# Low parts of the output weights by accumulating DMAs, token sums on VectorE, a third plain pair and more norm buffers in a hybrid attention/SSM/ConvFFN block on one Trainium2 core

## The chip, the cores and the metric

The kernel runs on one core of one Trainium2 chip. The metric is the device time of one execution in microseconds. The kernel before took 1517.89 us (median of three runs, 1514.3 to 1518.22); one further execution was taken with the hardware profiler, and all lines of the profile come from it. A difference under about 0.3% (4.5 us) cannot be told from no change for this kernel.

## The reference, cut to what matters

One layer over 16 meta tokens and 1024 sequence tokens of width 1024. The change lies in the second half: merging and output projection, second norm, and the first matrix of the gated ConvFFN.

```python
def _mixer(xn, ...):
    ...
    merged = g[..., :D_MODEL] * y_a + g[..., D_MODEL:] * y_s      # y_a = attention @ w_attn_out
    return merged @ w_o

def _conv_ffn(xn, w_up, conv_w, conv_b, w_down):
    hid = xn @ w_up                                   # 1024 -> 2 * 2816
    hp = jnp.pad(hid, ((0, 0), (CONV_WIDTH - 1, 0), (0, 0)))
    conv = conv_b + sum(hp[:, j:j + seq_len] * conv_w[j] for j in range(CONV_WIDTH))
    val, gate = jnp.split(conv, 2, axis=-1)
    return (jax.nn.silu(gate) * val) @ w_down

def reference(...):
    ...
    h = h + _mixer(_rmsnorm(h, norm_mix_g), ...)
    h = h + _conv_ffn(_rmsnorm(h, norm_ffn_g), ...)
    return _rmsnorm(h, norm_final_g)[:, N_META:]
```

## The kernel before, in words

**Split operands.** Everything is float32. A matrix operand is cut into a high part of reduced width (type `float32r`, written `hi`) and a low part `lo = x - hi`, and each product is three matmuls: hi·hi, hi·lo, lo·hi. A `hi` is a copy on ACT (or POOL); a `lo` is a subtraction of two SBUF tiles on VectorE (DVE) or POOL (`split_lo`, line 129), or else an ACT copy of `-hi` followed by a DMA from POOL's queue that adds the original from DRAM onto it (`lo_by_dma`, lines 133 to 136). All of the `split_lo` instructions carry line 129, all of those DMAs line 136, so they are told apart by tile names.

**Order of the work.** The program is written in a fixed order, and a scheduler that has a model of the engines orders the instructions of each engine from it. On the chip each engine takes its own list strictly in order: an instruction that waits holds back everything behind it on that engine. The same holds for the DMA queues of SP and POOL.

**Attention output and merge (lines 943 to 963).** For each of eight row blocks `i`, the weights of `w_attn_out` are split by `wchunk` (high part on POOL, line 149; low part on DVE) and multiplied with the attention output in three pieces of 342 tokens (lines 958 to 960). DVE multiplies with the gate (L961) and adds the SSM part (L962) into `merged[i]`, tile `mr`. After each block `out_forms` makes operands of the output projection.

**Output projection (lines 1008 to 1070).** `merged @ w_o` is done with seven half-size block products instead of eight (a Strassen-like scheme), in the order `p = 0, 4, 1, 5, 2, 3, 6`. Each product has four token blocks `t` of 12 matmuls of 512 columns (lines 1015 to 1017), `i` or `j` running over four row blocks of the operands. `out_weights` loads the weight combination of a product, 128 rows of 512 columns for each `j` (from `w_o` itself for p = 0, 4, 6; from tensors `to_d` in DRAM, summed earlier, for the others). `out_forms(p, j)` makes the four operand tiles of slot `j`: high and low part of the token side (`a`) and of the weight side (`b`). Before, all `lo` are subtractions: on POOL for p = 0, 4, 5 and on DVE for p = 1, 2, 3, 6. The slots are the eight quarters of the tiles `xhi` and `xlo` (p = 0, 5, 3 share `xhi`, p = 4, 2 share `xlo`) and four tiles `op` (p = 1, 6), so forms of a product can only be written when the product two or three places ahead has been read by PE. Small products for the two meta tokens (lines 994, 995) read the same weight slots. DVE adds each result from PSUM to `h2` or `u2` (L1021); after p = 2 POOL adds `u2` to three blocks of `h2` for each `t` (L1024).

**Second norm (`normed`, lines 1026 to 1031).** For each 128 tokens: square and sum on ACT (L170, the squares are written into the tile `xs`, of which there are two), a scale on DVE (L172), a power on POOL (L174), the product into `xs` on DVE (L179), eight transposes on PE (L187), high parts on ACT (L189), low parts on DVE (L129, `xlo<-sp` and `xlo<-tp`). Blocks 5 to 8 follow product 6's token blocks, then the meta rows (block 0), then blocks 1 to 4.

**Up projection.** The 22 pairs (a gate chunk and a value chunk of 128 columns of `w_up`) come in two kinds. `plain_pair` multiplies directly: 144 matmuls of about 342 columns (lines 1165 to 1167), accumulated in PSUM, evacuated by one ACT and two DVE instructions a piece (L1169, L1171) that apply the convolution's taps. Three banks are called `mm`, one `po`; a piece can start when an earlier piece has left its bank. Pair 0 is cut in two parts: first the tokens from 514 on (blocks 5 to 8), then the others. `block_pair` uses the seven-product scheme: 168 matmuls of 258 or 256 columns (lines 215 to 217) over sums of weight blocks, which POOL makes (`combine`, L1121), and over sums of token blocks. These token sums are made once (`xn_forms`, L1185 on POOL: high plus low part, 16 of them; then 16 subtractions, lines 254 to 258, and 16 low parts `t0l` to `t3l` on DVE) while plain pair 1 runs. Pairs 0, 1 and 21 are plain, 2 to 20 are block pairs. The conv outputs and `hid` go to DRAM and the down projection follows.

**Memory.** `pool` opens a stretch of SBUF on the left or the right side; a tile of a new pool waits for the last users of what lay there. `merged` and `wstream` (the `raw`, `whi`, `wlo` tiles) lie on the right and are closed after the last norm, where the pool `upw` of up-projection weights takes their place.

Of the kernel before, what the change touches and what calls it, by code (L numbers as in the profile page):

```python
# [19 lines left out]
P = 128  # L20
# [30 lines left out]
def block_kernel(ctx, tc, x, meta, g1, x0t, g1t, w_q, w_k, w_v, w_f, w_u, w_g, b_f, w_ao, lam_d, bw_d, cw_d,  # L51
# [86 lines left out]
    def wchunk(src, k, eng=None, act=False):  # L138
        raw = wp.tile([P, k, P], F, tag="raw", name="raw", padded_shape=[P, KD, P])
        ld = (GP if act else SY).dma_start(raw, src)  # L140
        if act:
            after(ld, late[0])
        hi = wp.tile([P, k, P], R, tag="whi", name="whi", padded_shape=[P, KD, P])
        lo = wp.tile([P, k, P], R, tag="wlo", name="wlo", padded_shape=[P, KD, P])
        if act:
            S.copy(hi, raw)
            lo_by_dma(lo, hi, src)
            return hi, lo
        GP.tensor_scalar(hi, raw, 1.0, 0.0, ALU.mult, ALU.add)
        split_lo(eng or V, lo, raw, hi)  # L150
        return hi, lo
# [25 lines left out]
    def norm_rows(pl, src, n, gB, xs):  # L177
        rs = norm_factor(pl, src, n, 3, xs)
        V.scalar_tensor_tensor(out=xs[:n], in0=src, scalar=rs[:n], in1=gB[:n], op0=ALU.mult, op1=ALU.mult)  # L179
# [708 lines left out]
    merged = [mp.tile([P, LQ], F, name=f"mr{i}") for i in range(KD)]  # L888
# [30 lines left out]
    def out_weights(p, q, pl, tag, bufs=2):  # L919

        t_ = pl.tile([P, 2, 512], F, tag=tag, name="wr", bufs=bufs)
        src = (o_block(*own_w[p]) if p in own_w else to_d[p])[256 * q:256 * q + 256]
        SY.dma_start(t_, src.rearrange("(c p) d -> p c d", p=P))
        wr[p, 2 * q], wr[p, 2 * q + 1] = t_[:, 0], t_[:, 1]

    def out_forms(p, j):
# [12 lines left out]
        for q, src in ((0, (a11, a11, a11, a21, a12, a22, a11)[p]), (2, wr.pop((p, j)))):  # L939
            S.copy(slot[q], src)  # L940
            split_lo(GP if p in (0, 4, 5) else V, slot[q + 1], src, slot[q])
# [6 lines left out]
    for i in range(KD):  # L948
# [5 lines left out]
        whi, wlo = wchunk(w_ao[i], 4)  # L954
# [80 lines left out]
    tags = {1: "raw", 5: "whi", 2: "wlo", 3: "raw", 6: "whi"}  # L1035
# [7 lines left out]

    operands(None)
# [29 lines left out]
    st_o.close()  # L1074
    st_w.close()
# [4 lines left out]

    st_r = ExitStack()
    fc = pool(st_r, "ffnc", side="right")

    cwt = fc.tile([P, 4, 2 * NFF], F, name="cwt")
    SY.dma_start(cwt, cwt_d)
# [7 lines left out]
    KH = KD // 2  # L1093
    rp = pool(st_r, "upw", side="right")
# [6 lines left out]

    def up_raw(m):
        raw = rp.tile([P, KD, P], F, tag="raw", name="raw", bufs=3)
        SY.dma_start(raw, w_up[m])
        return raw

    def ring():
        t_ = rp.tile([P, 2, KH, P], R, tag="sw", name="sw", bufs=8)
        return t_[:, 0], t_[:, 1]

    def split_q(src):
        hi, lo = ring()
        S.copy(hi, src)  # L1113
        split_lo(V, lo, src, hi)
        return hi, lo
# [34 lines left out]
    def plain_pair(c, parts=(QBLK,)):  # L1150
        res = []
        ws = {}
        for part, (m, tag) in ((part, mt) for part in parts for mt in ((NFF + c, "og"), (c, "ov"))):
            if m not in ws:
                raw = up_raw(m)
                ws[m] = [split_q(raw[:, KH * q:KH * q + KH]) for q in range(2)]
                res.append(conv_out(m, tag))
            w2, o = ws[m], res[len(ws) - 1 if len(ws) < 2 else int(m == c)]
# [23 lines left out]
    def xn_forms():  # L1182
        def whole(dst, r, h_, k):
            b = block(r, h_)
            GP.tensor_tensor(dst, b[0][:, k].bitcast(F), b[1][:, k].bitcast(F), ALU.add)  # L1185
# [7 lines left out]
    def block_pair(c):  # L1193
# [3 lines left out]
        down_weight_sums(c - 2, sums[n_])  # L1197
# [588 lines left out]
```

## Time and profile before

| | |
|---|---|
| Runs before, median of three | 1517.89 us (1514.3 to 1518.22) |
| Profiled execution, its time | 1517.67 us |
| Its span, first to last instruction | 1515.9 us |
| PE busy | 1447.7 us (96%) |
| DVE / ACT / POOL busy | 1093.1 / 697.6 / 782.2 us (72 / 46 / 52%) |
| Attention output and merge on PE | about 669 to 720 us |
| Output projection on PE | 719.7 to 810 us |
| Plain pairs 0 and 1 on PE | 811.7 to 882 us |
| Block pairs on PE | from about 882 us, 20.1 us each |

A row of the timeline reads: start, duration, engine, line, operation, out<-in, shape and type, how many were merged, and in brackets the idle time before it with what ended it. A row of the windows reads: the stretch, its length, then for each engine its busy time and the number of instructions, then the granted PE clock as a share of the full one, the mean busy share of the 16 DMA engines, and GB/s. Matmuls overlap in their recorded durations, so the pace of PE is read from starts or counts.

### The profile page before, as it was taken

The page shows a single profiled execution, that of the slowest core. Times are in us where ns is not written, and L with a number is a line of the kernel's source. Part 1 is how long each engine was busy: PE and PEld are TensorE (multiplying, and loading weights), DVE is VectorE, ACT ScalarE, POOL GpSimd, SP SyncE. Part 2 cuts the span into 40 slices and gives each one's busy share as a digit, 9 for nine tenths or more (in the row PEclk, how much of TensorE's full clock was granted, in tenths as well). Part 3 has the DMA queues.
Part 4 walks back from the last instruction along what each step waited for, and adds up shares of the span by engine and source line. Part 5 has one row for each costly group of instructions (what it writes and reads, how often), then busy time and mean ns, then how long its engine had stood idle before and what let it go on. Part 6 is the DMA issues. An engine that isn't in the chain of part 4 may idle for free.

```text
span 1515.9 us, 26588 instructions
## 1 busy us (share of the span) xinstructions
PE 1447.7 (96%) x9736; PEld 1363.6 (90%) x9736; DVE 1093.1 (72%) x2178; ACT 697.6 (46%) x1351; POOL 782.2 (52%) x866
## 2 busy tenths in 40 slices
PE   7999997999999999999998799999999999999997
PEld 6989997998999999998787799999999999878886
DVE  7878748871656676645777987888887774798785
ACT  6334665531546565540435444444444444444343
POOL 1411136760546555546852645555544326599766
PEclk9999999999999999999999899999999999999999
DMA  6365572551027422164533146676643214774413
GB/s 241 94 163 141 141 139 63 164 168 51 23 78 192 128 55 92 43 251 152 211 88 135 43 105 174 174 189 180 166 114 98 73 68 167 290 238 127 138 49 111
DMA packets 88150, 201.46 MB, mean 133 GB/s; under 512 B 14330, under 2 KB 25210, under 8 KB 87636
## 3 DMA queue, kind: packets, MB, share of 16 engines
q1 hardware_dynamic: 69956, 161.83, 32.7%
q0 software_dynamic: 11840, 27.28, 10.1%
q10 hardware_dynamic: 6224, 10.65, 1.9%
q8 instruction: 77, 1.26, 0.3%
q14 instruction: 53, 0.43, 0.1%
HBM read 160.65 MB, written 69.35 MB: 152 GB/s over the span
## 4 chain that ended last, share of the span: by engine, by line
PE 78%; DVE 9%; DMA 6%; issue 3%; POOL 2%; ACT 2%; SPq 0%; POOLq 0%; DVEq 0%; ACTq 0%
PE mm L155 4%; PE mm L157 4%; PE mm L156 4%; PE sp L215 4%; PE sp L216 4%; PE sp L217 4%; PE mm L215 3%; PE tp L215 3%; PE mm L217 3%; PE tp L216 3%; PE mm L216 3%; PE tp L217 3%; PE tp L752 2%; PE po L774 1%; PE po L773 1%
## 5 line engine op out<-in xcount | busy, mean ns | idle before, releaser
L155 PE MATMUL mm<-xhi,whi 128*128 128x342 f32 (+2 forms) x488 | 159.4, 327 | 1.0 <-DVE q L129 1.0
L157 PE MATMUL mm<-xhi,wlo 128*128 128x342 f32 (+2 forms) x488 | 158.3, 325 | 0.0
L156 PE MATMUL mm<-xlo,whi 128*128 128x342 f32 (+2 forms) x488 | 157.7, 324 | 0.0
L1144 POOL TENSOR_TENSOR ov<-ov,og 128x1024 f32<-128x1024 f32 x21 | 51.3, 2441 | 130.7 <-ACT og L1143 127.9
L129 DVE TENSOR_TENSOR sw<-sf,sw 128x512 fp32r<-128x512 f32 x76 | 70.7, 931 | 52.5 <-ACT sw L1113 52.5
L1113 ACT CAST sw<-sf 128x512 fp32r<-128x512 f32 x76 | 47.5, 625 | 112.1 <-POOL sf L1121 79.2
L155 PEld LDWEIGHTS mm<-xhi,whi 128*128 128x128 f32 x488 | 91.9, 188 | 2.1 <-PE sp L710 0.8
L157 PEld LDWEIGHTS mm<-xhi,wlo 128*128 128x128 f32 x488 | 91.8, 188 | 0.3
L156 PEld LDWEIGHTS mm<-xlo,whi 128*128 128x128 f32 x488 | 91.9, 188 | 0.2
L217 PE MATMUL mm<-xhi,sw 128*128 128x256 f32 (+1 forms) x304 | 85.5, 281 | 0.0
L215 PE MATMUL mm<-xhi,sw 128*128 128x256 f32 (+1 forms) x304 | 85.3, 281 | 0.0
L216 PE MATMUL mm<-xlo,sw 128*128 128x256 f32 (+1 forms) x304 | 85.2, 280 | 0.0
L759 ACT CAST th<-tp 128x256 fp32r<-128x256 f32 (+3 forms) x120 | 56.2, 472 | 61.8 <-PE tp L752 28.1
L129 DVE TENSOR_TENSOR tl<-tp,th 128x256 fp32r<-128x256 f32 (+3 forms) x120 | 65.2, 547 | 25.8 <-ACT th L759 24.4
L724 POOL TENSOR_SCALAR pt<-pt,nm 128x144 f32<-128x144 f32 (+4 forms) x72 | 51.6, 729 | 50.7 <-DVE nm L723 49.7
L1121 POOL TENSOR_TENSOR sf<-raw,sf 128x512 f32<-128x512 f32 x38 | 62.2, 1638 | 27.4 <-DVE sw L129 27.4
L1206 DVE SCALAR_TENSOR_TENSOR ov<-hv,cwt,ov 128x1024 f32<-128x1024 f32 x38 | 74.2, 1953 | 0.2
L1121 POOL TENSOR_TENSOR sf<-raw 128x512 f32<-128x512 f32 x38 | 49.9, 1314 | 45.9 <-DVE sw L129 21.7
L1113 ACT CAST sw<-raw 128x512 fp32r<-128x512 f32 x69 | 42.4, 620 | 58.9 <-PE sp L217 27.8
L722 ACT ACTIVATE pt<-pt,nm 128x144 f32<-128x144 f32 (+4 forms) x72 | 52.9, 735 | 27.3 <-DVE nm L721 26.9
L715 DVE CUSTOM_DVE_ANT_0 pt<-sp,fb 128x328 f32<-128x328 f32 (+8 forms) x112 | 46.4, 430 | 19.5 <-PE sp L710 11.3
L129 DVE TENSOR_TENSOR sw<-raw,sw 128x512 fp32r<-128x512 f32 x69 | 57.6, 842 | 3.5 <-ACT sw L1113 2.6
(693 smaller groups left out, 5733.9 us busy)
## 6 DMA issues: line engine op xcount, KB each, us to landing
raw<-in_w_up_dram SPq DMA_DIRECT2D x44, 512.0 KB, 3.7
t_d<-in_w_dn_dram POOLq DMA_DIRECT2D x44, 256.0 KB, 6.9
ar<-a_d SPq DMA_DIRECT2D x44, 256.0 KB, 4.9
wr<-t_d SPq DMA_DIRECT2D x44, 256.0 KB, 2.9
a_d<-ov SPq DMA_DIRECT2D x21, 512.0 KB, 2.6
wr<-in_w_dn_dram SPq DMA_DIRECT2D x33, 256.0 KB, 3.4
t_d<-in_w_dn_dram SPq DMA_DIRECT2D x22, 256.0 KB, 4.7
t_d<-t_d SPq DMA_DIRECT2D x22, 256.0 KB, 4.7
```

Of the source, the lines that this page charges most:

```text
L129: return eng.tensor_tensor(out_, src, hi.bitcast(F), ALU.subtract)
L155: yield PE.matmul(ps, whi[:, i, :], ahi[:, i], start=(i == 0), stop=False)
L156: yield PE.matmul(ps, whi[:, i, :], alo[:, i], start=False, stop=False)
L157: yield PE.matmul(ps, wlo[:, i, :], ahi[:, i], start=False, stop=(i == k - 1))
L215: PE.matmul(ps, a[0][:, i], bh, start=(i == 0 and not joins), stop=False, skip_group_check=True)
L216: PE.matmul(ps, a[0][:, i], bl, start=False, stop=False, skip_group_check=True)
L217: PE.matmul(ps, a[1][:, i], bh, start=False, stop=(i == kh - 1), skip_group_check=True)
L722: S.activation(pt[:n, :kc], pt[:n, :kc], AF.Exp, bias=nm[:n, 1:2], scale=0.125, accum_out=nm[:n, 2:3])
L759: S.copy(th[:kn, z:tw], tp[:kn, z:tw])
L1113: S.copy(hi, src)
L1121: sums.append(GP.tensor_tensor(f_, a, b, op))
L1206: V.scalar_tensor_tensor(out=o, in0=h_[:, j:SEQ + j], scalar=cwc(j, m), in1=o, op0=ALU.mult, op1=ALU.add)
```

## The change

1. **Low parts of the output weights.** In `out_forms` the low part of the weight side (`slot[3]`) is no longer a subtraction but `lo_by_dma`: an ACT copy of `-hi` and an accumulating DMA of 256 KB in POOL's queue, from `w_o` or `to_d`. There are 28 of each (seven products, four `j`).
2. **High parts of `w_attn_out`** are copied by ACT instead of POOL (`copy=True`), the low parts stay on DVE.
3. **Norm buffers.** The squares go into a tile of their own (`sf`, two), the result of the meta rows is written in place, and the results of blocks 7 and 2 go into the third `raw` buffer of the up weights.
4. **First pair's weights ahead.** `merged` and `wstream` are closed before product 2 and `upw` is opened there; the weights of pair 0 are loaded and split in that place.
5. **Token sums** (`whole`) run on DVE, not on POOL.
6. **Pair 2 is a plain pair;** the block pairs are 3 to 20, and the sums of the down weights follow one pair later (`c - 3`).

```diff
-    def wchunk(src, k, eng=None, act=False):
+    def wchunk(src, k, eng=None, act=False, copy=False):
...
+        if copy:
+            S.copy(hi, raw)
+            split_lo(V, lo, raw, hi)
+            return hi, lo
         GP.tensor_scalar(hi, raw, 1.0, 0.0, ALU.mult, ALU.add)
         split_lo(eng or V, lo, raw, hi)
...
-    def norm_rows(pl, src, n, gB, xs):
-        rs = norm_factor(pl, src, n, 3, xs)
+    def norm_rows(pl, src, n, gB, xs, sq=None):
+        rs = norm_factor(pl, src, n, 3, sq)
...
-        for q, src in ((0, (a11, a11, a11, a21, a12, a22, a11)[p]), (2, wr.pop((p, j)))):
-            S.copy(slot[q], src)
-            split_lo(GP if p in (0, 4, 5) else V, slot[q + 1], src, slot[q])
+        a_ = (a11, a11, a11, a21, a12, a22, a11)[p]
+        S.copy(slot[0], a_)
+        split_lo(GP if p in (0, 4, 5) else V, slot[1], a_, slot[0])
+        b_, src = wr.pop((p, j))
+        S.copy(slot[2], b_)
+        lo_by_dma(slot[3], slot[2], src)
...
-        whi, wlo = wchunk(w_ao[i], 4)
+        whi, wlo = wchunk(w_ao[i], 4, copy=True)
...
     def normed(c, dst, n):
-        xs = n2.tile([P, D], F, tag="xs", name="xs", bufs=2)
-        norm_rows(n2, dst, n, g2B, xs)
+        if c:
+            pl, tag, bufs = (rp, "raw", 3) if c in (7, 2) else (n2, "xs", 2)
+            xs = pl.tile([P, D], F, tag=tag, name="xs", bufs=bufs)
+        else:
+            xs = dst
+        sq = rp.tile([P, D], BF, tag="sf", name="sq", bufs=2)
+        norm_rows(n2, dst, n, g2B, xs, sq)
...
     for p in (0, 4, 1, 5, 2, 3, 6):
+        if p == 2:
+            st_o.close()
+            st_w.close()
+            fc = pool(st_r, "ffnc", side="right")
+            cwt = fc.tile([P, 4, 2 * NFF], F, name="cwt")
+            rp = pool(st_r, "upw", side="right")
+            early = {m: pair_weights(m) for m in (NFF, 0)}
+            SY.dma_start(cwt, cwt_d)
         for t in range(4):
             out_product(p, t)
...
         def whole(dst, r, h_, k):
             b = block(r, h_)
-            GP.tensor_tensor(dst, b[0][:, k].bitcast(F), b[1][:, k].bitcast(F), ALU.add)
+            V.tensor_tensor(dst, b[0][:, k].bitcast(F), b[1][:, k].bitcast(F), ALU.add)
...
-        down_weight_sums(c - 2, sums[n_])
+        down_weight_sums(c - 3, sums[n_])
...
-    plain_pair(0, ([(514, 256), (770, 254)], [(0, 258), (258, 256)]))
+    plain_pair(0, ([(514, 256), (770, 254)], [(0, 258), (258, 256)]), early)
     xn_forms()
     plain_pair(1)
-    for c in range(2, NFF - 1):
+    plain_pair(2)
+    for c in range(3, NFF - 1):
         block_pair(c)
```

How the order of instructions moves, at three places. The line numbers of the changed kernel are 4 to 21 higher (L1021 is L1029, L1024 is L1032, L1171 is L1191, L1185 is L1205).

DVE in the output projection, from the last result of product 4 to the first results of product 1 (`h<-h,sp`); `xlo` are the low parts of product 2's operands, `mr` its token side and `wr` its weight side. Before:

```order
L129 TENSOR_TENSOR xlo<-mr_8510,xlo 128x512
L1021 TENSOR_TENSOR h_9082<-h_9082,po 128x512
L129 TENSOR_TENSOR xlo<-mr_8511,xlo 128x512
L129 TENSOR_TENSOR xlo<-wr,xlo 128x512 x4
L1021 TENSOR_TENSOR h_9082<-h_9082,sp 128x512
```

In the changed kernel:

```order
L1029 TENSOR_TENSOR h_9090<-h_9090,po 128x512
L1007 TENSOR_TENSOR ml<-ml,tp 2x512
L129 TENSOR_TENSOR xlo<-mr_8510,xlo 128x512
L129 TENSOR_TENSOR xlo<-mr_8511,xlo 128x512
L1029 TENSOR_TENSOR h_9090<-h_9090,sp 128x512
```

The four weight-side subtractions no longer stand ahead of the first result of product 1.

POOL after product 5, where product 3's weight sides are made (`to_d_85` is the weight combination of product 3) and `u` is added to `h`. Before, POOL had only the twelve additions there:

```order
L1000 TENSOR_TENSOR hm<-hm,ml 2x512
L1024 TENSOR_TENSOR h_9082<-h_9082,u_9076 128x512 x6
L1024 TENSOR_TENSOR h_9082<-h_9082,u_9077 128x512 x6
```

In the changed kernel:

```order
L136 DMA xhi<-to_d_85 128x512 x2
L1032 TENSOR_TENSOR h_9090<-h_9090,u_9084 128x512 x3
L136 DMA xhi<-to_d_85 128x512 x2
L1032 TENSOR_TENSOR h_9090<-h_9090,u_9084 128x512 x3
L1032 TENSOR_TENSOR h_9090<-h_9090,u_9085 128x512 x6
```

The DMAs for `j` = 2 and 3 stand behind three additions that need the first result of product 2.

DVE at the end of the norm: the last low parts of block 4, then the evacuation of pair 0's first part, the piece `og 128x256` being the one whose bank the second part takes first (two instructions of that form empty it). Before:

```order
L129 TENSOR_TENSOR xlo<-tp,xhi 128x4x128
L1171 SCALAR_TENSOR_TENSOR og<-mm,cwt,og 128x256
L1171 SCALAR_TENSOR_TENSOR og<-mm,cwt,og 128x254
L1171 SCALAR_TENSOR_TENSOR og<-mm,cwt,og 128x256
```

In the changed kernel:

```order
L129 TENSOR_TENSOR xlo<-tp,xhi 128x4x128
L1205 TENSOR_TENSOR fa<-xhi,xlo 128x514
L1205 TENSOR_TENSOR fb<-xhi,xlo 128x514
L1205 TENSOR_TENSOR fa<-xhi,xlo 128x514
L1191 SCALAR_TENSOR_TENSOR og<-mm,cwt,og 128x256
L1205 TENSOR_TENSOR fa<-xhi,xlo 128x514 x2
L1191 SCALAR_TENSOR_TENSOR og<-mm,cwt,og 128x254
L1191 SCALAR_TENSOR_TENSOR ov<-mm,cwt,ov 128x256
L1191 SCALAR_TENSOR_TENSOR ov<-po,cwt,ov 128x254
L1191 SCALAR_TENSOR_TENSOR og<-mm,cwt,og 128x256
```

Five token sums and three other evacuations now stand ahead of the instruction that frees that bank. Further on, PE has 18 matmuls of the first block pair's second product (`sp`) between the first and the second value piece of plain pair 1, that is before plain pair 2.

More of the change, by code (lines that the diff above doesn't have):

```diff
@@ L887, in block_kernel @@
     mp = pool(st_o, "merged", side="right")
[L888 removed]
+    merged = [mp.tile([P, LQ], F, tag=f"mr{i}", name=f"mr{i}") for i in range(KD)]
     st_m = ExitStack()
@@ L1034, in block_kernel, with up_raw, ring, split_q @@
     after_of = {None: (1,), 0: (5,), 4: (2,), 5: (3, 6)}
-    tags = {1: "raw", 5: "whi", 2: "wlo", 3: "raw", 6: "whi"}
+    def up_raw(m):
+        raw = rp.tile([P, KD, P], F, tag="raw", name="raw", bufs=3)
+        SY.dma_start(raw, w_up[m])
+        return raw
+    def ring():
+        t_ = rp.tile([P, 2, KH, P], R, tag="sw", name="sw", bufs=8)
+        return t_[:, 0], t_[:, 1]
+    def split_q(src):
+        hi, lo = ring()
+        S.copy(hi, src)
+        split_lo(V, lo, src, hi)
+        return hi, lo
+    def pair_weights(m):
+        raw = up_raw(m)
+        return [split_q(raw[:, KH * q:KH * q + KH]) for q in range(2)]
+    tags = {1: "raw", 5: "whi", 2: "wlo", 3: "raw", 6: "wlo"}
     def operands(p):
```

35 lines of the change are left out of this document (9 added, 26 removed).

## Prediction

> **What bounds the kernel now.** I read the page first, then the chain and the waits of PE over the stretch that the change touches (685 to 900 us), then windows with the granted clock, then the timelines of DVE, POOL and ACT around each wait.
>
> ```profile
> span 1515.9 us, 26588 instructions
> PE 1447.7 (96%) x9736; PEld 1363.6 (90%) x9736; DVE 1093.1 (72%) x2178; ACT 697.6 (46%) x1351; POOL 782.2 (52%) x866
> ```
>
> PE is busy for all but 68 us, so only what removes a wait of PE, or its matmuls, shortens the time. In the stretch of the change PE waited four times over 1 us:
>
> ```profile
> PE mm L1165 <- DVE og L1171: 11.2, 2, 8.5
> PE mm L958 <- POOL whi L149: 3.4, 1, 3.4
> PE sp L1015 <- DVE h L1021: 2.8, 1, 2.8
> PE sp L187 <- DVE xs L179: 2.6, 1, 2.6
> ```
>
> Behind each, PE ran slowly (next to last three columns: granted clock, DMA share, GB/s):
>
> ```profile
> 690.00:694.00 4.00, 4.00 (x18) 3.85 (x19) 3.65 (x4) 0.62 (x1) 2.19 (x3) 0.64 0.23 67
> 757.00:762.00 5.00, 5.00 (x16) 3.92 (x17) 3.55 (x6) 2.98 (x6) 1.27 (x1) 0.66 0.08 21
> 834.00:840.00 6.00, 5.82 (x28) 5.85 (x29) 4.84 (x9) 0.98 (x2) 4.57 (x5) 0.53 0.01 3
> 872.00:877.00 5.00, 4.95 (x17) 4.98 (x18) 4.64 (x8) 2.07 (x4) 4.42 (x4) 0.50 0.29 47
> ```
>
> Length times the missing clock is what each cost besides the wait: 1.4, 1.7, 2.8 and 2.5 us. So there are 20.0 us of waits and 8.4 us of slow clock, 28.4 us, to win at most.
>
> **The long wait: token sums beside plain pair 1.** DVE works on the token forms while PE wants its banks emptied:
>
> ```profile
> 853.03 0.68 DVE L257 TENSOR_TENSOR fa<-fa 128x514 f32<-128x514 f32 x1
> 853.63 0.68 DVE L129 TENSOR_TENSOR t0l<-fa,t0h 128x514 fp32r<-128x514 f32 x1
> ...
> 865.35 1.75 DVE L257 TENSOR_TENSOR fa<-fa 128x514 f32<-128x514 f32 x1
> ```
>
> POOL's timeline after the first place and at the second:
>
> ```profile
> 856.98 1.69 POOL L1121 TENSOR_TENSOR sf<-raw,sf 128x512 f32<-128x512 f32 x1 [4.82 <-DVE sw L129]
> ...
> 864.83 3.40 POOL L1185 TENSOR_TENSOR fa<-xhi,xlo 128x514 f32<-128x514 f32 x2
> ```
>
> The same subtraction takes 0.68 us at 853, the next starting 0.60 us after it, while POOL is idle (4.82 us before 856.98); and it takes 1.75 at 865, where POOL's sums run. Only behind such rows comes the evacuation that PE waits for. On DVE alone the 16 sums cost about 16 × 0.6 = 9.6 us, and the 32 subtractions beside them come at the short pace. With 16 + 32 at 0.6 (29 us), 8 weight splits at 0.6 (4.8) and the evacuations left of pairs 0 and 1 (about 10), DVE needs some 44 us. The PE work beside it now includes plain pair 2, so I take the wait of 8.5 and its 2.5 us of slow clock as gone: **11.0 us** (8 to 11). That there is cover: the forms are done about 20 us before the first full block product. But 18 of its matmuls stand ahead inside plain pair 1, where the third quarter of one token form is due; by my sum DVE and PE get there within 1 us of each other, so each microsecond of lateness there is a wait.
>
> **The third plain pair.** PE's timeline has the pace of a plain pair, ACT's timeline and the view of line 224 that of the block pairs:
>
> ```profile
> 878.24 0.32 PE L1165 MATMUL mm<-xhi,sw 128*128 128x342 f32 x1
> ...
> 880.12 0.32 PE L1165 MATMUL mm<-xhi,sw 128*128 128x342 f32 x1
> ```
> ```profile
> 885.42 0.37 ACT L224 COPY c<-mm 128x256 f32<-128x256 f32 x1 [0.64 <-PE mm L217]
> ```
> ```profile
> L224 ACT COPY c<-mm x12: 352/370/375, 884.4 to 985.7; 128x258 f32<-128x258 f32 x6, 128x256 f32<-128x256 f32 x6
> ```
>
> Twelve matmuls of 342 take 1.88 us, 0.157 each; 144 take 22.6. Two copies L224 belong to each block pair, so from the second to the twelfth lie five pairs: (985.7 − 885.4) / 5 = 20.1 us. The swap costs **2.5 us** (2 to 3), on PE's path with no cover.
>
> **The norm.** Before, the last low part of block 4 came at 832.9 and the first bank of pair 0 was emptied by three evacuations after it:
>
> ```profile
> 832.17 0.69 DVE L129 TENSOR_TENSOR xlo<-tp,xhi 128x512 fp32r<-128x512 f32 x1 [0.16 <-ACT xhi L189]
> 832.78 1.25 DVE L1171 SCALAR_TENSOR_TENSOR og<-mm,cwt,og 128x256 f32<-128x256 f32 x3
> ```
>
> PE's side: the start of pair 0 in the timeline, four transposes in the chain, and a window of its matmuls:
>
> ```profile
> 811.67 0.36 PE L1165 MATMUL mm<-xhi,sw 128*128 128x258 f32 x1
> ```
> ```profile
> 801.08 0.44 PE tp L187 x4
> ```
> ```profile
> 810.00:820.00 10.00, 10.00 (x86) 9.67 (x85) 6.43 (x12) 5.49 (x12) 1.09 (x2) 1.00 0.16 66
> ```
>
> With the squares in a tile of their own ACT no longer waits for `xs`, and four weight splits fewer lie ahead, so the transposes reach PE in time. From 811.7, PE has 96 matmuls at 10 / 86 = 0.117 (11.2 us) and 4.2 us of transposes (32 at 0.11, and 8 short ones): it runs dry at 827.1. The last transposes stand 16 matmuls earlier, 825.2; an ACT copy and a DVE subtraction of some 0.6 each end at 826.5. Then the list has five token sums (5 × 0.6) and five evacuations (5 × 1.25 / 3 = 2.1): the bank is free at 831.6, not at 834.0. So of the two waits (2.6 and 2.7) one of 4.5 is left, with the clock's 2.8, and pair 0's second part starts **2.4 us** earlier (0 to 8, the upper end if no wait is left).
>
> **The output projection.** The 2.8 us wait came from DVE:
>
> ```profile
> 749.34 6.86 DVE L129 TENSOR_TENSOR xlo<-wr,xlo 128x512 fp32r<-128x512 f32 x4
> 756.12 0.67 DVE L1021 TENSOR_TENSOR h<-h,sp 128x512 f32<-128x512 f32 x1
> ```
>
> Those four are now DMAs, so this wait and its clock, 4.5 us, go. What is late next is product 3. Its slots are free when product 5 ends; call that 0. Rows for the chain are a window of the matmuls, two copies of ACT, POOL's additions, and the landing times of accumulating DMAs by line (L136, then L1139):
>
> ```profile
> 770.00:780.00 10.00, 10.00 (x46) 8.29 (x45) 7.19 (x12) 5.41 (x10) 2.94 (x3) 1.00 0.39 116
> ```
> ```profile
> 770.22 0.62 ACT L940 CAST xhi<-mr 128x512 fp32r<-128x512 f32 x1 [6.74 <-PE tp L1016]
> 770.75 0.62 ACT L940 CAST xhi<-wr 128x512 fp32r<-128x512 f32 x1
> ```
> ```profile
> 777.06 18.70 POOL L1024 TENSOR_TENSOR h<-h,u 128x512 f32<-128x512 f32 x12 [18.25 <-DVE u L1021]
> ```
> ```profile
> L136 POOL DMA_DIRECT2D wlo<-in_w_g_dram x7: 862/872/1222, 73.1 to 171.4; - x7
> ...
> DMA to landing us min/median/max: 6.3/7.3/13.1
> ```
> ```profile
> DMA to landing us min/median/max: 4.8/6.9/8.9
> ```
>
> PE reaches product 3 after product 2 (48 matmuls and 8 small ones at 0.22, four of them done earlier): about 12.0, and its slot `j` = 2 at 13.4. ACT's twelve operations at 0.53 start about 1.5 early and end at 4.8. On POOL the three additions wait for product 2's first result, 4.7, and take 3 × 1.56 or less: the DMA for `j` = 2 is issued at 8.6 to 9.4. The last landing row is that of the accumulating DMAs of 256 KB into DRAM (L1139, 4.8 to 8.9, median 6.9); the row above it is of 512 KB into SBUF (7.3). Mine are 256 KB into SBUF: 4.8 at best, 6.9 at worst in a quiet queue. They land at 13.4 to 16.3: a wait of 0 to 3 us, with clock 0 to 5. Taken: 1.6 and 0.4 for the clock, near the short end, since the queue is quiet there. Product 5's land by then; its `j` = 3 within 1 us. **2.5 us** gained (−3 to 4.5). The 28 `-hi` copies of ACT (28 × 0.53 = 15 us) lie in its idle time, 46% busy, and cost nothing by themselves.
>
> Two rules beside these rows. The Trainium skill, "SBUF — State Buffer", section "SBUF: two separate sides", warns that a DMA issued from GpSimd cannot write its descriptors while VectorE runs an instruction in a two-port mode; the trace has 0.87 us for the median issue and 1.22 for the longest (row L136), so hardly any of it. By that rule each of the two late DMAs would stand for one DVE instruction of 0.6 us, and the gain would be 1.2 us smaller. The Trainium skill, "TensorE: Matmul & The Clock Gate", section "What's actually happening", has the clock halved after at least one idle window of about 3.4 us; the trace differs, 0.66 after a wait of 2.8. By that rule the wait at product 3 costs no clock, and the gain is 0.4 us larger.
>
> **The attention output.** PE waited for POOL's `whi` (the second row of the waits), which stood in POOL's list behind weight-side subtractions; they ended at 688.05:
>
> ```profile
> 684.30 3.75 POOL L129 TENSOR_TENSOR xlo<-wr,xlo 128x512 fp32r<-128x512 f32 x3
> ```
>
> The window just before, and POOL's DMA queue on the page (packets, MB, share):
>
> ```profile
> 676.00:680.00 4.00, 4.00 (x27) 4.00 (x26) 1.49 (x3) 1.76 (x3) 4.00 (x4) 1.00 1.04 401
> ```
> ```profile
> q0 software_dynamic: 11840, 27.28, 10.1%
> ```
>
> Both leave POOL. But the new copy stands in ACT's list behind the copies of the fourth load `wr`, and here all 16 DMA engines are full. A megabyte of POOL's queue costs 0.101 × 1515.9 / 27.28 = 5.6 us of all engines; four new DMAs (1.05 MB) are 5.9 us. They can push that load, and with it the copy, back by up to 5.9 us. Of 3.4 + 1.4 = 4.8 us I take **3.0** (0 to 4.8).
>
> Edits with one answer: weights of pair 0 ahead (DVE split them during the last products before, too), meta rows in place, and `down_weight_sums` one pair later, which still ends two pairs before the last: zero. The scheduler also reorders some of the down projection's operands; I take zero and widen the range by 2.
>
> **The sum.** 11.0 + 2.4 + 2.5 + 3.0 − 2.5 = 16.4 us. Against the profiled execution's own 1517.67 (span 1515.9 and 1.8 around it; 0.2 under the median) this is **1501.3 us**.
>
> **The rivals.**
>
> *Late DMAs.* If they land in 10 us rather than 5 to 6 (13.1 is the longest row above, in full engines), product 3 waits 5 us more, product 5 about 3, the attention output wins nothing: 16.4 − 11 = 5.4, **1512 us**. For it: engines full at 676. Against: a share of 0.39 at 770. Chance 0.15.
>
> *DVE becomes the bound: slower.* If the short pace at 853 had another cause than POOL's silence, each token operation takes up to the 1.75 of the row at 865, 1.1 more; I take 0.8. Of the 48, 37 stand ahead of the 18 matmuls inside plain pair 1 in DVE's list: 37 × 0.8 = 30 us late there, PE's list is in order, and the cover of pair 2 comes behind it. Net 16.4 − 30 = −14: **1531 us**. It decides from a delay of 16.4 us there, 0.44 for each of the 37. Against: at 853 DVE ran at 0.60 while POOL had nothing, and that is the state the change makes. Chance 0.05.
>
> *More than forecast.* If evacuation and sums fall the other way on DVE and no wait is left in the norm, and product 3's DMAs are in time: + 5 + 2 + 1.5, **1492 us**. Chance 0.14.
>
> *The change does not do what it says,* that is, waits move one for one (a wait at product 3, one before the second part of pair 0, one at the 18 matmuls): **1517 us**. Chance 0.04.
>
> **How the numbers follow.** The forecast has 0.62, its own range being 1496 to 1507. Range of 8 in 10: it and the larger part of 1492 and 1512: 1493 to 1511. About 0.3%, 4.5 us, is what a measurement can tell from no change. Faster by more than that: 0.62 + 0.14 + most of the late DMAs 0.12 = 0.88. Same: 0.04 + 0.03 = 0.07. Slower: 0.05.
>
> **What would show it.** Right: no wait of PE on `og` over 5 us in plain pairs 0 to 2, full-width DVE subtractions there at 0.6 us apart, none at `h<-h,sp`, a wait of 0 to 3 us at the start of product 3 on a DMA, one of about 4 before the second part of pair 0, the first block pair about 6 us later than the first one before, though one pair further on. Wrong: a clock of 0.5 in plain pair 1, or PE waiting for `t1l`, or `whi` late again at 686.

## The result, and the profile after

The changed kernel takes 1506.4 us median against 1518.1 before, a ratio of 0.9931 (95% interval 0.9909 to 0.9952). Measured again beside the first experiments it was 1508.5 against 1516.1, 0.9962 (0.9949 to 0.9975). So it is faster by 7.6 to 11.7 us, where 16.4 were forecast. Its page begins:

```profile
span 1503.6 us, 26570 instructions
PE 1447.3 (96%) x9712; PEld 1364.3 (91%) x9712; DVE 1058.6 (70%) x2173; ACT 713.6 (47%) x1384; POOL 746.8 (50%) x854
```

PE's waits in the stretch of the change (640 to 930 us):

```profile
PE mm L966 <- ACT whi L150: 5.9, 1, 5.9
PE mm L1185 <- DVE og L1191: 4.6, 1, 4.6
PE sp L221 <- DVE sw L129: 3.2, 1, 3.2
PE po L778 <- DVE tl L129: 0.6, 2, 0.3
```

Three of the old waits are gone: the one in the output projection (`h<-h,sp`), the one of 8.5 us in plain pair 1 and the one on `xs` in the norm. The other wait of the norm, before pair 0's second part, has grown from 2.7 to 4.6, and the wait on `whi` from 3.4 to 5.9. A new one of 3.2 stands inside pair 1. Windows over the three places, 685 (`whi`), 828 (pair 0's second part) and 860 (`sw`) (the last three columns are granted clock, DMA share, GB/s):

```profile
685.00:690.00 5.00, 1.17 (x3) 0.94 (x4) 0.69 (x1) 0.62 (x1) 1.93 (x2) 0.50 1.08 283
690.00:695.00 5.00, 5.00 (x19) 5.00 (x19) 3.72 (x6) 1.24 (x2) 0.88 (x1) 0.50 0.84 215
...
825.00:830.00 5.00, 1.36 (x6) 1.39 (x7) 5.00 (x12) 0.62 (x1) 0.00 (x0) 0.83 0.01 3
830.00:835.00 5.00, 5.00 (x37) 5.00 (x36) 5.00 (x10) 2.72 (x5) 0.00 (x0) 0.83 0.00 0
...
860.00:865.00 5.00, 4.35 (x31) 4.36 (x32) 5.00 (x10) 1.71 (x3) 0.00 (x0) 1.00 0.00 0
```

At 685 all DMA engines are full (share 1.08) and PE stands or runs at half clock for 10 us. From 825 to 865 VectorE (third pair of figures) is busy without a pause.

The difference by stage, from the first matmul of each stage in PE's timeline. Gains are in us; "again" is the second profile of the changed kernel, read against the one profile of before:

| stretch | forecast | first profile | again |
|---|---|---|---|
| up to the attention output (nothing changed there) | 0 | 3.0 | 2.5 |
| attention output (`w_ao`) | 3.0 | −3.5 | −3.0 |
| output projection | 2.5 | 4.5 | 4.5 |
| pair 0, first part (the norm) | 2.4 | 1.6 | 1.6 |
| pair 0's second part to pair 21 (long wait 11.0, third pair −2.5) | 8.5 | 5.9 | 4.2 |
| pair 21 and down projection | 0 | 0.1 | −1.3 |
| behind PE's last matmul | 0 | 0.7 | 0.7 |
| sum | 16.4 | 12.3 | 9.2 |

Two lines fall short by more than 2 us: the attention output, by 6.0 to 6.5, and the stretch of the token forms, by 2.6 to 4.3. The first line can't be put down to the change, since PE's list is the same up to there. In the two profiles of the changed kernel and those of the ten experiments built on it PE reached the attention output anywhere from 662.1 to 668.6 us. The two profiles with the old code have it at 668.7 and 668.5, at the end of that spread. Whether a part of these 2 to 3 us belongs to the change stays open.

### The profile page after: what moved, and what is told of

The parts are those of the page before. It is cut to its first block, busy times and chain, and to the rows that moved or that the text cites. A ratio compares the mean times of both kernels' runs of the same rounds, so it can differ in the third digit from the quotient of the medians.

```text
span 1503.6 us, 26570 instructions
## 1 busy us (share of the span) xinstructions
PE 1447.3 (96%) x9712; PEld 1364.3 (91%) x9712; DVE 1058.6 (70%) x2173; ACT 713.6 (47%) x1384; POOL 746.8 (50%) x854
## 4 chain that ended last, share of the span: by engine, by line
PE 78%; DVE 8%; DMA 6%; POOL 3%; issue 2%; ACT 2%; SPq 0%; POOLq 0%; DVEq 0%; ACTq 0%
PE mm L161 4%; PE mm L159 4%; PE mm L160 4%; PE sp L221 4%; PE sp L219 4%; PE sp L220 4%; PE mm L219 3%; PE tp L219 3%; PE mm L221 3%; PE tp L220 3%; PE tp L221 3%; PE mm L220 3%; PE tp L756 2%; PE po L778 2%; PE po L777 2%
## 5 line engine op out<-in xcount | busy, mean ns | idle before, releaser
L129 DVE TENSOR_TENSOR sw<-sf,sw 128x512 fp32r<-128x512 f32 x72 | 66.2, 919 | 50.6 <-ACT sw L1059 50.6
L1141 POOL TENSOR_TENSOR sf<-raw,sf 128x512 f32<-128x512 f32 x36 | 58.7, 1632 | 49.3 <-DVE sw L129 48.3
L221 PE MATMUL mm<-xhi,sw 128*128 128x258 f32 (+1 forms) x288 | 81.0, 281 | 0.0
L219 PE MATMUL mm<-xhi,sw 128*128 128x258 f32 (+1 forms) x288 | 80.8, 281 | 0.0
L220 PE MATMUL mm<-xlo,sw 128*128 128x258 f32 (+1 forms) x288 | 80.7, 280 | 0.0
L756 PE MATMUL tp<-ident,pt 128*128 128x128 f32 (+1 forms) x360 | 58.2, 270 | 0.1
```

What stands on the lines that cost most here:

```text
L129: return eng.tensor_tensor(out_, src, hi.bitcast(F), ALU.subtract)
L219: PE.matmul(ps, a[0][:, i], bh, start=(i == 0 and not joins), stop=False, skip_group_check=True)
L220: PE.matmul(ps, a[0][:, i], bl, start=False, stop=False, skip_group_check=True)
L221: PE.matmul(ps, a[1][:, i], bh, start=False, stop=(i == kh - 1), skip_group_check=True)
L756: PE.transpose(tp[:kn, o:o + n], p_[:n, k0:k0 + kn], ident[:n, :n])
L1141: sums.append(GP.tensor_tensor(f_, a, b, op))
```

## Experiments: the attention output

ACT's timeline of the changed kernel has the `whi` that PE waited for:

```profile
682.96 0.60 ACT L945 CAST xhi<-mr 128x512 fp32r<-128x512 f32 x1
688.16 0.62 ACT L150 CAST whi<-raw 128x512 fp32r<-128x512 f32 x1 [4.60 <-DMA raw<-in_w_ao_dram]
```

ACT had been idle for 4.6 us: the copy did not stand behind others, its input had not landed. `raw` has two buffers, and the fourth of the eight copies reads the fourth load. SP's timeline has its issue; then come the view of the tile `raw` (640 to 705 us) with the times from issue to landing, and the DMA view of 650 to 700 us and, last, of 671.05 to 688.1 us:

```profile
671.05 0.33 SPq L140 DMA_DIRECT2D raw<-in_w_ao_dram  x1
```
```profile
DMA to landing us min/median/max: 2.7/4.5/18.2
```
```profile
q1 hardware_dynamic: 3824, 10.76, 60.0%
q0 software_dynamic: 1152, 2.10, 22.8%
```
```profile
q0 software_dynamic: 822, 1.52, 48.2%
```

The load was issued at 671.05, and the copy could start at 688.1, 17.0 us later. The 18.2 us belong to the next load, whose copy stands at 692.8. (The view has no landing for the load at 671.05, nor for its counterpart in the trace of before, where the longest on record was 5.3.) POOL's queue (q0) moved 2.10 MB in 650 to 700, for 22.8% of 50 us of all 16 engines: 11.4 us, 5.4 per MB. While the late load was under way it took 48.2% of 17.0 us, 8.2 us. The theory (transfers) against the rival (the copy's place on ACT), by three runs.

**again**: the changed kernel, unaltered.

> The changed kernel once more, beside the others of this group. In its first profile PE reached the first matmul of L966 3.2 us sooner than the kernel before reached it, although PE's instructions are the same up to there. If that is only the spread of executions, this profile reaches it within 2 us of either side of that, and the ratio stays within 0.991 to 0.995; if it is a property of the changed program, it comes within 0.5 us of the first profile. The waits of PE on `whi` (5.9 us), on `og` before pair 0's second part (4.6) and on `sw` inside pair 1 (3.2) come back within 1 us each.

Measured: 1508.5 us, the waits 6.5, 4.6 and 2.6, the attention output reached at 666.2. The waits belong to the kernel. The ratio, 0.9962, is outside the 0.991 to 0.995 that was expected. The start came within 0.5 us of the first profile, but the other runs spread over 6.5 us, so this is not the property that the expectation allowed for.

**ao_sub**:

```
         S.copy(slot[2], b_)
-        lo_by_dma(slot[3], slot[2], src)
+        if p in (0, 4):
+            split_lo(GP, slot[3], b_, slot[2])
+        else:
+            lo_by_dma(slot[3], slot[2], src)
```

> The weight-side low parts of products 0 and 4 are POOL subtractions again, as before the change; the `whi` copy stays on ACT. Theory (transfers): the eight accumulating DMAs of these two products, 2.1 MB, fill the DMA engines and push the load `raw` from 4.5 to 18.2 us; without them PE waits at most 1 us on `whi`, the granted clock at 685 to 695 us is 0.95 or more instead of 0.50, and the kernel is 7 to 9 us faster than the changed one. Rival (ACT's list): the copy is late because it stands behind others on ACT; then the wait stays between 3 and 6 us and the time within 2 us. The scheduler also moves 14 of the 18 matmuls that stand early in plain pair 1 to a later place here, which may take up to 3 us off the wait on `sw`; so the verdict is read from the wait on `whi`, not from the total alone.

Measured: 1497.9 us, ratio 0.9886 (0.9867 to 0.9904), 10.5 us below the changed kernel beside it. Its waits in the same stretch, and the clock (line numbers are 3 higher here):

```profile
PE mm L1188 <- DVE og L1194: 6.1, 2, 4.6
PE mm L969 <- DVE ga L972: 1.0, 1, 1.0
```
```profile
685.00:690.00 5.00, 4.02 (x26) 3.74 (x25) 4.97 (x7) 0.42 (x1) 3.38 (x3) 1.00 0.25 74
690.00:695.00 5.00, 5.00 (x34) 5.00 (x33) 4.66 (x6) 1.45 (x3) 2.82 (x3) 1.00 0.52 158
```

No wait on `whi`, a clock of 1.00, and the stage is 46.6 us long: 54.5 and 54.0 with the DMAs, 51.0 before. The load that took 17.0 us is issued at 671.31 here and copied at 681.44, 10.1 us later:

```profile
681.44 0.62 ACT L150 CAST whi<-raw 128x512 fp32r<-128x512 f32 x1 [0.55 <-DMA raw<-in_w_ao_dram]
```

Another 1.5 to 3.3 us are gained from pair 0's second part to pair 21 (420.0 us against 421.5 and 423.3), where the scheduler has moved 14 of the 18 early matmuls and the wait inside pair 1 is 1.5; that the move alone did this no run shows.

**ao_pool**: `wchunk(w_ao[i], 4, copy=True)` becomes `wchunk(w_ao[i], 4)`.

> `whi` of the attention output is copied on POOL again, and all accumulating DMAs stay. Theory (transfers): the load is late, whoever copies it: PE still waits 4 to 8 us on `whi`, the load still lands 15 us or more after its issue at worst, time within 2 us of the changed kernel. Rival (ACT's list): POOL has nothing ahead of the copy now, the wait is 1 us or less and the kernel 6 to 8 us faster.

Measured: 1511.9 us, 0.9972 (0.9961 to 0.9983), 3.4 above the changed kernel beside it, where up to 2 were expected; the stage 55.4 us. The wait has only changed its owner:

```profile
PE mm L966 <- POOL whi L153: 6.6, 1, 6.6
```

With all three the cause is shown: the accumulating DMAs of products 0 and 4 delay a load that PE needs at once. The rival falls.

## Experiments: VectorE beside the token forms

VectorE's timeline of the changed kernel at the end of the norm, and 25 us later; then POOL's:

```profile
823.43 0.69 DVE L1205 TENSOR_TENSOR fa<-xhi,xlo 128x514 f32<-128x514 f32 x1
824.03 0.69 DVE L1205 TENSOR_TENSOR fb<-xhi,xlo 128x514 f32<-128x514 f32 x1
824.64 0.69 DVE L1205 TENSOR_TENSOR fa<-xhi,xlo 128x514 f32<-128x514 f32 x1
825.24 0.48 DVE L1191 SCALAR_TENSOR_TENSOR og<-mm,cwt,og 128x256 f32<-128x256 f32 x1
825.64 1.29 DVE L1205 TENSOR_TENSOR fa<-xhi,xlo 128x514 f32<-128x514 f32 x2
...
828.01 0.48 DVE L1191 SCALAR_TENSOR_TENSOR og<-mm,cwt,og 128x256 f32<-128x256 f32 x1
...
845.94 1.77 DVE L262 TENSOR_TENSOR fb<-fb,fa 128x514 f32<-128x514 f32 x1
...
849.63 2.89 DVE L258 TENSOR_TENSOR fb<-fa 128x514 f32<-128x514 f32 x1
...
859.92 0.68 DVE L129 TENSOR_TENSOR sw<-sf,sw 128x512 fp32r<-128x512 f32 x1
```
```profile
845.54 1.62 POOL L1141 TENSOR_TENSOR sf<-raw,sf 128x512 f32<-128x512 f32 x1
849.33 2.63 POOL L1164 TENSOR_TENSOR ov<-ov,og 128x1024 f32<-128x1024 f32 x1 [2.17 <-DVE ov L1191]
```

Three things are to be seen. The five sums stand ahead of the evacuation at 828.01 that PE waits for, 0.6 us apart. Where POOL works, one subtraction takes 1.77 and one 2.89 us, so POOL is not silent here. And the split at 859.92, a low part of the first block pair's weights, is the one on which PE waited 3.2 us, for 18 matmuls of that pair that stand inside plain pair 1. The Trainium skill, "SBUF — State Buffer", section "Who interferes with whom", says that a VectorE tensor-tensor operation with both inputs in SBUF and a GpSimd operation that reads SBUF exclude each other, and that the second to start waits for the first. The rows agree: the subtraction begun at 849.63 ends 0.6 us after POOL's product.

**hold**: the first block pair's T2 product only behind plain pair 2.

```
+                if hold is not None and i == 0 and b is T2:
+                    after(mm, hold)
...
+    hold = plain_pair(2)
```

> The T2 product of the first block pair may start only behind the last matmul of plain pair 2. Theory (place in PE's list): the 3.2 us wait on `sw` is there only because 18 matmuls of this product stand inside plain pair 1, where VectorE has not got to their operands; behind pair 2 the operands are there, the wait goes, and the kernel is 2.5 to 3.5 us faster than the changed one. Rival (VectorE is the bound of the whole stretch): the wait comes back on `og` in plain pairs 1 and 2, and the time stays within 1 us.

Measured: 1511.6 us, 0.9968 (0.9956 to 0.998), against 0.9962 for the changed kernel: nothing gained. The wait on `sw` is gone, and one of 4.1 on an evacuation has taken its place:

```profile
PE mm L1187 <- DVE og L1193: 8.7, 2, 4.6
```

In VectorE's list token forms still stand ahead of pair 1's evacuations; the rival was right.

**glue**: `(V if c == NFF - 1 else GP)` becomes `(V if c in (0, NFF - 1) else GP)`.

> The changed kernel with the product of pair 0's two halves (L1164, 2.6 us on POOL, during which one VectorE subtraction took 2.9 instead of 0.6 us) on VectorE instead. Theory (POOL's instructions slow VectorE in the stretch that the forecast called silent): VectorE saves 2.2 us and gets 1.2 more, so the wait on `sw` inside pair 1 falls by about 1 us, to 1.5 to 2.2. Rival (only the amount of VectorE work counts): the wait grows by 1.2, to 3.8 or more. The total moves by less than 2 us either way; the verdict is read from the wait.

Measured: the wait is 0.9 us, less than the theory had; 1504.5 us, 0.993 (0.991 to 0.995).

```profile
PE sp L221 <- DVE sw L129: 0.9, 1, 0.9
```

VectorE got 1.2 us more work and was sooner done. The wait is 1.7 to 2.3 us shorter, but not all of that is VectorE's. Counted from the start of pair 0's second part, the wait ends after 30.7 us, against 32.0 in the first profile and 32.2 in again: 1.3 to 1.5 us are VectorE's, near the 1 of the theory. The rest against the first profile is that PE, half clocked for longer, reached the place 1.0 later.

**two_plain**: pair 2 is a block pair again.

```
-    plain_pair(2)
-    for c in range(3, NFF - 1):
+    for c in range(2, NFF - 1):
...
-        down_weight_sums(c - 3, sums[n_])
+        down_weight_sums(c - 2, sums[n_])
```

> Pair 2 is a block pair again (and the sums of the down weights start one pair earlier), the token sums stay on VectorE. As the forecast has it, the third pair is the cover: without it PE waits for the token forms in plain pair 1 or the first block pair for 5 to 8 us, and the time is 2.5 to 6 us above the changed kernel's. Rival (not needed): VectorE is through with the forms at 871 us, just after the end of plain pair 1 at 867; the wait is 2 us or less and the time 0 to 2.5 us below the changed kernel's.

Measured: 1501.8 us, 0.9914 (0.99 to 0.9928), against 0.9962 for the changed kernel. From pair 0's second part to pair 21 it takes 418.1 us; 421.5 and 423.3 with the third pair, 427.4 before. These 3.4 to 5.2 us are more than the rival's 0 to 2.5. All its waits in the stretch of the change:

```profile
PE mm L966 <- ACT whi L150: 6.5, 1, 6.5
PE mm L1185 <- DVE og L1191: 4.6, 1, 4.6
PE po L778 <- DVE tl L129: 0.6, 2, 0.3
PE mm L219 <- ACT c L228: 0.6, 1, 0.6
```

There is no wait left in plain pair 1, though no third pair follows. The last low part of the forms starts at 869.8, 4.3 us after the first block pair, whose later products are the first to need it. The scheduler has also spread 32 matmuls of the first block pair over plain pair 1, 12 of them among its first pieces, where the changed kernel has 18 in one place; so it is the kernel as built that shows it: the third plain pair was not needed.

**b_sums**: the kernel before, with only `GP.tensor_tensor` in `whole` turned into `V.tensor_tensor`.

> The kernel before with one part of the change: the token sums on VectorE instead of POOL. By the forecast's price (0.6 us on VectorE while POOL is silent, against 1.75 beside POOL's sums) VectorE is done earlier although it has 16 instructions more: the 8.5 us wait of plain pair 1 shrinks by 3 us or more, and the time falls by 3 to 9 us. Rival (work moved onto the later engine): 16 x 0.6 = 9.6 us more on VectorE, the wait stays over 7 us, the time within 2 us of the kernel before. Up to the attention output PE's instructions are those of all the other kernels: if the spread of executions made the 3 us there, this profile reaches the first matmul of L958 anywhere from 665.7 to 668.7 us.

Measured: 1510.8 us, 0.9974 (0.9964 to 0.9985), 4.2 us less. In its profile the stretch from pair 0's second part to pair 21 is 418.8 us, 8.6 shorter than before, and the 8.5 us wait is gone:

```profile
PE mm L1165 <- DVE og L1171: 6.5, 1, 6.5
PE mm L958 <- POOL whi L149: 3.3, 1, 3.3
```

The 6.5 us are another wait: the one before pair 0's second part, 2.7 before, where the sums now stand ahead of the evacuations. It took back 3.8. The theory was right: this one part of the change wins most of the long wait alone, and loses at the norm.

**order**: the sums of the four token quarters stand behind evacuations 7, 15, 19 and 23 of VectorE (counted from 0).

```
+            after(s_, evacs[{0: 7, 1: 15, 2: 19, 3: 23}[k]])
...
-    xn_forms()
+    xn_forms((0, 1))
     plain_pair(1)
+    xn_forms((2, 3))
```

> The token sums of the four quarters stand behind evacuations in VectorE's list: quarter 1 behind the eight of pair 0's first part, quarter 2 behind the eight of its second part, quarters 3 and 4 behind two groups of pair 1. The work is the same. Theory (order of VectorE's list): between 823 and 871 us VectorE does token forms for a product that is due only at 892, ahead of evacuations that PE waits for at once; with the evacuations first the 4.6 us before pair 0's second part fall to 1.5 or less, the 2.6 to 3.2 us on `sw` inside pair 1 go too, and the time is 5 to 8 us below the changed kernel's. Rival (VectorE's throughput): every microsecond that PE is given early is asked back, as when the T2 product was held; the waits come back on `t0l` to `t3l` or `og` later on, and the time stays within 1.5 us.

Measured: 1500.4 us, 0.991 (0.9895 to 0.9925). In the profile the wait of 4.6 is 0.8, and one of 1.8 is left on `t1l`:

```profile
PE sp L220 <- DVE t1l L129: 1.8, 1, 1.8
PE mm L1187 <- DVE og L1193: 0.8, 1, 0.8
```

From pair 0's first matmul to pair 21 it takes 439.8 us against 442.4 and 444.2, a gain of 2.6 to 4.4. That is about half of the 5 to 8 of the theory and more than the 1.5 of the rival (by the ratios the kernel is 3 to 8 us below the changed one). Pair 0's first part wins 3.8 us; the stretch behind it takes 422.7, between 1.2 more and 0.6 less than in the two profiles of the changed kernel.

**Together.** *order_ao* is ao_sub and order, *two_ao* is ao_sub and two_plain; *two_ao_evac* and *two_ao_evac1* put the first quarter's sums behind evacuation 7 and evacuation 1 as well.

> Both edits that the runs so far point to: the low parts of products 0 and 4 by subtraction (10.5 us below the changed kernel in the first group) and the token sums behind the evacuations. If the two waits are separate (theory), the gains add: 15 to 18 us below the changed kernel, 1.5% below the kernel before. If VectorE's throughput bounds the stretch from the norm to the first block pair (rival), the second edit adds nothing: 9 to 11 us.

> The changed kernel without two of its parts: no third plain pair, and the weight-side low parts of products 0 and 4 by subtraction. Both alone were faster than the changed kernel, by about 10 and by 7 us against the runs beside them. If they are separate (theory), the sum is 14 to 18 us below the changed kernel, a ratio to the kernel before of 0.983 to 0.988. If the third pair was not needed only because the late start left VectorE time (rival), PE waits on `og` or the token forms for 3 us or more in plain pair 1, and the time is within 2 us of ao_sub's 1498.

> As two_ao, and the token sums of the first quarter stand behind the eight evacuations of pair 0's first part. Theory (order of VectorE's list): the 4.6 us wait before pair 0's second part and its slow clock shrink to 1.5 us, 3 to 5 us below two_ao. Rival (VectorE is the bound up to the first block pair, and no plain pair lies behind as cover now): the waits come back in plain pair 1, within 1.5 us of two_ao.

> As two_ao_evac, but the first token sums stand behind the second evacuation step of the first bank only, so that they start about 2 us earlier. Theory: the bank that PE waits for is free as early, so the wait before pair 0's second part is 1.5 us as well, and the token forms are ready earlier: 0 to 2 us below two_ao_evac. Rival (VectorE's order between the other banks decides): another bank frees later, a wait of 2 us or more before the second part, and the time is 1 to 3 us above two_ao_evac.

Measured, with the time of the kernel before beside each, and two stretches of the profile (pair 0's first part; its second part to pair 21):

| kernel | us | before | ratio (95%) | pair 0, first part | second part to pair 21 |
|---|---|---|---|---|---|
| ao_sub | 1497.9 | 1516.1 | 0.9886 (0.9867 to 0.9904) | 20.9 | 420.0 |
| order_ao | 1494.8 | 1514.9 | 0.9867 (0.985 to 0.9884) | 17.1 | 420.7 |
| two_ao | 1493.9 | 1515.2 | 0.9853 (0.983 to 0.9876) | 20.9 | 418.1 |
| two_ao_evac | 1497.9 | 1515.2 | 0.9882 (0.9862 to 0.9902) | 17.1 | 423.7 |
| two_ao_evac1 | 1497.0 | 1515.2 | 0.9875 (0.9856 to 0.9895) | 17.1 | 422.8 |

two_ao and order_ao are the best, 20 to 21 us below the kernel before and not to be told apart. By the changed kernel's two ratios (0.9931 and 0.9962) two_ao is 12 to 17 and order_ao 10 to 14 us below it: order_ao's sum falls short of the 15 to 18 of its theory, and over ao_sub its 3 us are within the intervals. two_ao agrees with its theory, with the ratio expected and no wait of its rival's. Its one wait over 1 us between 640 and 930 us is the 4.6 before pair 0's second part:

```profile
PE mm L1188 <- DVE og L1194: 4.6, 1, 4.6
PE mm L219 <- ACT c L228: 0.8, 1, 0.8
```

With evacuations first (the last two rows) pair 0's first part is 3.8 us shorter, as forecast, and the rest up to pair 21 is 4.7 to 5.6 longer, with small waits on token forms and, from 869.7 us on, half the clock for 6.8 us:

```profile
PE tp L219 <- ACT t0h L264: 1.5, 1, 1.5
PE tp L220 <- DVE t0l L129: 1.0, 1, 1.0
PE sp L220 <- DVE t1l L129: 0.8, 1, 0.8
```

(two_ao_evac1's waits.) They stand in the first block pair, not in plain pair 1 where the rival had them, and the two kernels are not to be told apart. So without the third pair these edits moved PE's wait and did not remove it. With the third pair behind, order, which moves the sums of all four quarters, gained 2.6 to 4.4 us; that this is because the forms then have 22.6 us longer is an inference.

## Why the prediction was right, and where it was not

*Faster, and inside the range:* right. The size was too large by 5 to 9 us. There is some luck in how near it came: of the 12.3 and 9.2 us of the two profiles, 3.0 and 2.5 lie ahead of the attention output, where the sum had nothing; the stages that it named gave 8.5 and 7.3, and 0.8 and −0.6 lie behind them.

*Attention output, 3.0: the step that failed.* "They can push that load, and with it the copy, back by up to 5.9 us" named the mechanism, took its price as the end of a range whose worst was no gain, and was about the wrong load. What came late was `raw`, the weights that PE needs in this stage, and eight DMAs ran beside it, not four: they took 8.2 us of all engines while it was under way, and it took 17.0 us instead of 10.1. The stage became 3.0 to 3.5 us longer. Without the eight it is 4.4 shorter than before, so the waits that leave POOL were priced well. Of the prediction's signs of being wrong this one came: `whi` late again at 686.

*Long wait, 11.0: mechanism right, size off.* VectorE's subtractions do come 0.6 us apart. The term measured 6.7 to 8.4 (4.2 to 5.9 and the third pair's 2.5). "By my sum DVE and PE get there within 1 us of each other" was wrong by 2 us, and the price that the prediction put on such a miss (each microsecond a wait) was right. It was a split of the weights that came late, not the token form that the prediction named; that one, `t1l`, is next in VectorE's list. VectorE was late because POOL was not silent: the one POOL instruction that glue moved accounts for 1.3 to 1.5 us.

*Third pair, 2.5:* the size is right (hold's 18 block pairs take 359.6 us, 19.98 each, against 22.6), its use is not. "The PE work beside it now includes plain pair 2" counted cover that stands behind the matmuls that wait; two_plain shows that none was needed. The check "about 6 us later" had an error of its own: 22.6 − 16.4 is the first block pair's delay only if the swap is free; with its own terms it is 20.1 − 16.4 = 3.7. Measured were 10.7 (892.7 against 882.0).

*Norm, 2.4:* a wait of 4.5 was forecast for the reason seen above, five sums and five evacuations; it is 4.6. PE ran dry 16.3 us after pair 0's start, where the working had 15.4 (827.1 − 811.7), and the bank was free 0.8 later than forecast too: 1.6 gained instead of 2.4.

*Output projection, 2.5:* it is 4.5, against the one profile of before, in every run with the change. Product 3 starts 11.9 us after product 5's end as forecast (12.0). The DMA for `j` = 2 is issued 7.9 us after that end (8.6 to 9.4 forecast) and lands 4.3 later (4.8 to 6.9 forecast): at 12.2, when the slot is due at 13.4. So no wait at all, the upper end of the gain, was the value to take. About 1.6 of the 4.5 are a slow clock that the old code does not always have: in b_sums, with the same wait of 2.8 us there, the clock stayed at 1.00, and the stage took 90.4 us, against 92.0 in the profile of before and 87.5 with the change. The issues on POOL took longer than the 1.22 us at most in the trace of before:

```profile
L136 POOL DMA_DIRECT2D xlo<-to_d x4: 1189/1704/2222, 752.9 to 754.5; - x4
```

These four start 0.54 us apart and take 1.19, 1.53, 1.88 and 2.22 us, so they end 0.88 apart: each stands behind the one before it. No product waits for them, and they show no delay by VectorE; whether the rule on descriptors that the prediction weighed ever acts here stays open.

*Rivals.* "Late DMAs" came true in the attention output alone, and there it cost more than the rival had, a loss instead of no gain. "DVE becomes the bound" came true without its price: VectorE is busy throughout from 823 to 869 us, but mostly at its fast pace, and the kernel is faster. "Waits move one for one" holds for hold and for the evacuations in two_ao_evac. The reordered down projection stayed within the ±2 us allowed.

## What to carry to other kernels

Moving work from an engine to an accumulating DMA takes it off that engine and puts it among the loads that run at the time: where the DMA engines are full already, find the load that PE needs next and count every new transfer against it. A cover counts only if it stands ahead of the first instruction that would wait, in the list of the waiting engine. Where one engine is busy throughout a stretch, putting its results in another order can just move the wait; here it gained clearly only with another plain pair behind.

## What the runs showed of the hardware

The accumulating DMAs of POOL's queue cost 5.4 us of all 16 engines per MB between 650 and 700 us; the plain transfers of q1 beside them cost 60.0% of 50 us for 10.76 MB, 2.8 per MB. Over the whole kernel it is 5.6 (POOL's queue) and 3.0:

```profile
q1 hardware_dynamic: 69956, 161.83, 32.6%
q0 software_dynamic: 15872, 34.63, 13.0%
```

How long PE waits doesn't say what the clock does behind it. Behind the 3.2 us on `sw` the changed kernel ran on at 1.00 (860 to 865, above); in again, at the same place, it ran at half the clock after a wait of 2.6; and in order after 1.8. The traces show what decides. In all fourteen the granted clock changes only on a grid of 3.41 us steps, whose place differs from one execution to the next. Windows cut on that grid, of the changed kernel, again and order:

```profile
855.60:859.00 3.40, 1.85 (x13) 1.64 (x11) 3.40 (x7) 1.87 (x4) 0.00 (x0) 1.00 0.00 0
859.00:862.40 3.40, 1.75 (x14) 1.75 (x15) 3.40 (x7) 0.62 (x1) 0.00 (x0) 1.00 0.00 0
```
```profile
857.40:860.80 3.40, 0.81 (x7) 0.60 (x5) 3.40 (x8) 1.34 (x3) 0.00 (x0) 1.00 0.00 0
860.80:864.20 3.40, 3.40 (x16) 3.40 (x17) 3.40 (x7) 1.06 (x1) 0.00 (x0) 0.50 0.00 0
```
```profile
876.90:880.30 3.40, 1.51 (x12) 1.26 (x11) 3.40 (x6) 2.22 (x5) 3.00 (x3) 1.00 0.12 31
880.30:883.70 3.40, 3.40 (x14) 3.40 (x15) 3.40 (x7) 0.96 (x3) 0.00 (x1) 0.50 0.97 149
```

In the changed kernel the edge of the grid cuts the wait, and PE is idle for 1.5 us of one step and 1.7 of the next; in again and order one step holds 2.6 and 1.9 us of idle time, and the next is at half clock. Over the whole of the fourteen traces, each of the 90 full-clock steps in which PE was idle for 1.92 us or more was followed by one at half clock, and none of the 5814 with less than 1.30; between the two it went both ways (45 not, 11 so). The ends of matmuls are modelled in the profile, so the idle times are good to some tenths of a microsecond.

The Trainium skill, "TensorE: Matmul & The Clock Gate", section "What's actually happening", lets the clock fall after at least one idle window of about 3.4 us, and has that window run freely. The traces agree with the free-running window; the length does not fit, 1.9 us of idle time in a step were enough.
